# A two-layer hybrid trunk on one core: merges as 512-column products, a beginning by quarters, and overlapping GLA heads

## The chip, the cores and the metric

The kernel runs on one core of a Trainium2 chip, alone. The metric is the device time of one execution in microseconds (us): the median of several runs.

## The reference

The reference is the backbone of a diffusion generator, two layers deep, over 256 context tokens and 256 latent tokens of width 1024. Each layer normalises and modulates its input, projects it once, feeds three mixers that run in parallel, merges them by gates, and ends with an MLP:

```python
def modulate(x, g, shift, scale):
    return rms_norm(x, g) * (1 + scale) + shift
# a layer: one input projection, split into
#   x, y             -> RG-LRU: conv, sigmoid gates, a scan in each direction, times gelu(y)
#   q, k, v, r, z    -> GLA: 4 heads, chunks of 64, both directions; decay gates from z
#   q, k, v          -> attention with 8 query and 2 key/value heads, rotary
#   gates            -> sum over branches of sigmoid(gate_b) * (branch_b @ W_b)
# then an output projection, a gated residual, and a squared-ReLU MLP
    u = jnp.sqrt(-jnp.expm1(2.0 * log_a)) * (i * xc)          # RG-LRU
    scores = jnp.einsum('nbhid,nbhjd->nbhij', qc * jnp.exp(b - b_mid), kc * jnp.exp(b_mid - b))   # GLA
```

Shift and scale come from a product of the conditioning vector with `mod_w`. Only the latent tokens of the last layer are output.

## The kernel before, in words

**Products.** Activations lie transposed: 128 channels on the partitions, up to 512 tokens in the columns (0 to 255 context, 256 to 511 latent). Each fp32 matrix is split into a high part rounded to the matmul's format and the rest, so that each product is three: high by high, high by low, low by high. `weight` loads a 128x1024 tile of weights, casts the high part on ACT (L200, `wh`) and subtracts on DVE (L201, `wl`), two or three weights ahead. `gemm` makes one 128-row output of 8 blocks, 24 products in a PSUM tile `mm`, of which there are four. `gemm_pair` takes an activation whose high and low parts lie beside each other, 256 columns each, so that one 512-column product makes two of the three, and a 256-column product the third; the two halves of its output must be added afterwards. `gemm_tok` makes GLA's V with tokens on the partitions, in four `mm` tiles at once.

**Order.** The scheduler issues each engine's instructions in the order in which the program calls them, but for pieces raised by a priority (weights, transfers of `mod_w`). Every engine then goes through its list in order: an instruction that waits holds up all that stand behind it on its engine. Layer 0 computes all 512 tokens; in layer 1 (`last`) the query side has only the 256 latent columns (`c0` is 256).

**A layer's beginning.** For layer 0 the norm's shift and scale come in four quarters (`mod_half`): a transfer of 2 MB (`mod_load`), products in `mx` tiles, a copy on ACT, a transpose, then an addition on DVE into `modT` (L319). `norm_apply` then makes two of the eight input blocks, from which the first products of the layer start.

**RG-LRU.** Eight blocks of 128 channels, in pairs: `lru_conv`, `lru_gates` (four products L526, activations L527 and L531), `lru_decay` (L538), one square root over a pair (L630), and `lru_scan` on DVE (L545 to L555, with a cast on ACT by L293 behind it). In between stand products of y (`gate_y`).

**GLA.** `gla_z` makes z (L568, with its weight split in `wzs`, L294). `gla_gates(h)` makes the head's log decays from z: products L598, then on ACT L601, L604 (exp) and L605 (ln). `gla(h)` makes K and Q (copied out by L653 and L656), V, then for each direction: exponentials, multiplications on DVE (L677 to L710), scores (L715, L717), and the state's update; a transpose of the decayed K waits for a copy (L775 for L767); R's products and the head's result (L851 follows L841) come last. `merge(b, i)` multiplies one block of a branch's output with its weight, computes the gate's product, and adds (L787 to L792); the merges of branch 1 and 2 in layer 1 have 256 columns.

Which gla step stands where is written out in the program: before, the gates of head 0 come after the last pair's scan, K, Q and V of each head at that head's beginning.

Of the kernel before, what the change touches and what calls it, by code (L numbers as in the profile page):

```python
# [15 lines left out]
F32 = mybir.dt.float32  # L16
# [14 lines left out]
WSPB, EBB, G2B, WRB = 3, 1, 3, 3  # L31
# [6 lines left out]
GZP, G0P = 2, 6  # L38
# [66 lines left out]
def trunk_kernel(ctx: ExitStack, tc: tile.TileContext, out: bass.AP, d: dict):  # L105
# [48 lines left out]
    c8 = const.tile([128, KT, 2], F32, name="c8")  # L154
# [9 lines left out]
    pick = const.tile([128, 2, 32], F32, name="pick")  # L164
    G.memset(pick, 0.0)
    for b in range(2):
        G.memset(pick[:, b, b:b + 1], 1.0)
# [6 lines left out]
    th = const.tile([128, KT, 2], F32, name="th")  # L174
# [100 lines left out]

    def gemm_tok(l, c, hh, hl, ts):
# [44 lines left out]
    def mods(l, us, pace, nd=KT):  # L321
# [5 lines left out]
        def load(u, j, k):  # L327
            with tc.high_priority(M_A):
                t = tmp()
                nc.sync.dma_start(t, d["mod_w"][l, u][:, k, 512 * j:512 * j + 512])  # L330
            return t
# [9 lines left out]
        for u, j in halves:  # L341
            bs = (0, 1) if l == 0 or u < 2 else (1,)
            acc = [tmp() for _ in bs]
            terms = [(pick[:, b, :], a) for a, b in zip(acc, bs)]
# [22 lines left out]
    def mod_load(l, u, h, tag):  # L367

        t = yp.tile([128, KT, 2, 256], F32, name="modw", tag=tag)
        src = d["mod_w"][l, u]  # L370
        if u < 2:
            nc.sync.dma_start(t, src.rearrange("p k (h c) -> p k h c", h=2)[:, :, :, 256 * h:256 * h + 256])
        else:
            nc.sync.dma_start(t.rearrange("p k h c -> p k (h c)"), src[:, :, 512 * h:512 * h + 512])
        return t

    def mod_half(l, u, h, t):
        dsts = (4 * u + 2 * h, 8 + 4 * u + 2 * h) if u < 2 else (8 * u + 4 * h, 8 * u + 4 * h + 2)
        for _ in mod_cols(l, 128, lambda k: (cs[:, k, :], lambda c: t[:, k, c // 256, c % 256:c % 256 + 128]), KT,
                          dsts):  # L380
            pass
# [55 lines left out]

    hn1 = norm_mul(0, 1)
    mq = [mod_load(0, q // 2, q % 2, ("yh", "yl")[q % 2]) for q in range(WQ)]
    first = [weight(0, "in", O_LY + 128 * i, hi="V", ahead=0) for i in range(2)]  # L440
    mq += [mod_load(0, q // 2, q % 2, ("yh", "yl")[q % 2]) for q in range(WQ, 4)]
    st = norm_stats(x1, 0)
    for q in range(4):
        mod_half(0, q // 2, q % 2, mq[q])
        norm_apply(0, 1, x1, 0, T, st, hn1, range(2 * q, 2 * q + 2))


    c2 = const.tile([128, NL, 2, 16], F32, name="c2")
    lam = const.tile([128, NL, 16], F32, name="lam")
    la = const.tile([128, NL, 16], F32, name="la")  # L450
    lb = const.tile([128, NL, 16], F32, name="lb")
    lc = const.tile([128, NL, 16], F32, name="lc")
    lo_, hi_ = PCOLS["lam"]
    V.tensor_copy(lam, par[:, :, lo_:hi_])
    S.activation(la, lam, AF.Abs)
    S.activation(la, la, AF.Exp, scale=-1.0)
    V.tensor_scalar(lb, la, 2.0, None, op0=ALU.add)
    V.reciprocal(lb, lb)
    V.tensor_tensor(la, la, lb, op=ALU.mult)
    V.tensor_tensor(lb, la, la, op=ALU.mult)  # L460
    V.tensor_scalar(lc, lb, 1.0 / 17, 1.0 / 15, op0=ALU.mult, op1=ALU.add)
    for n in (13, 11, 9, 7, 5, 3, 1):
        V.tensor_tensor(lc, lc, lb, op=ALU.mult)
        V.tensor_scalar(lc, lc, 1.0 / n, None, op0=ALU.add)
    V.tensor_tensor(lc, lc, la, op=ALU.mult)
    V.tensor_scalar(lam, lam, -1.0, 0.0, op0=ALU.mult, op1=ALU.max)
    V.scalar_tensor_tensor(lam, lc, 2.0, lam, op0=ALU.mult, op1=ALU.add)
    V.tensor_scalar(c2[:, :, 0, :], lam, -4.0, None, op0=ALU.mult)
    V.tensor_scalar(c2[:, :, 1, :], lam, 2.0, None, op0=ALU.mult)


    habx = const.tile([128, NL, 32], F32, name="habx")
    lo_, _ = PCOLS["ab"]
    _, hi_ = PCOLS["xb"]
    V.tensor_scalar(habx, par[:, :, lo_:hi_], 0.5, None, op0=ALU.mult)

    for l in range(NL):
# [22 lines left out]
        def gate_y(i):  # L500
            w = first[i] if l == 0 and i < 2 else weight(l, "in", O_LY + 128 * i, hi=E_LYH)
            ps = gemm(w, hh, hl, c0)
            ge[i] = x[:, i, :256] if last else tmp()
            S.activation(ge[i], ps, AF.Gelu_apprx_tanh)
# [52 lines left out]

        def gla_z():


            wz = tmp1(F32, (128, KT, 32))
            nc.sync.dma_start(wz, d["wz"][l])
            wzs = t2.tile([128, KT, 64], F32R, name="wzs", tag="t2")
            split_to(wzs[:, :, :32], wzs[:, :, 32:], wz)
# [50 lines left out]

        LYS = LYS0, LYS1
# [29 lines left out]
        v2 = {}  # L646

        def gla(h):
            bs = gla_gates(h) if h else gates0

            pk = gemm(weight(l, "in", O_GK + 128 * h), hh, hl, 0)
            k_ = tmp()
            cp(E_K)(k_, pk)  # L653
            pq = gemm(weight(l, "in", O_GQ + 128 * h), hh, hl, c0)
            q_ = tmp()
            S.activation(q_[:, c0:], pq, AF.Copy, scale=128.0 ** -0.5)  # L656
            if h % 2 == 0:
                for t, ps in gemm_tok(l, O_GV + 256 * h, hh, hl, range(4)).items():
                    for a in range(2):
                        v2[h + a, t] = tmp1()  # L660
                        cp(E_V)(v2[h + a, t], ps[:, 256 * a:256 * a + 256])
            v_ = [v2.pop((h, t)) for t in range(4)]

# [4 lines left out]
            pts, qhs = [], []  # L668
            for dd in range(2):
# [59 lines left out]
                kt = tmp()  # L729
                if dd == 0:  # L730
                    cp(E_KT)(kt[:, :384], pkt[:, :384])
                else:
                    S.copy(kt[:, :256], pkt[:, :256])
                    S.copy(kt[:, 384:], pkt[:, 384:])
                cur = None
# [32 lines left out]
            for j in range(2):  # L768
                pr = gemm(weight(l, "in", O_GR + 256 * h + 128 * j), hh, hl, c0)
                y = tmp()  # L770
                S.activation(y[:, c0:], pr, AF.Tanh, scale=0.5)
                V.scalar_tensor_tensor(y[:, c0:], y[:, c0:], 1.0, pr, op0=ALU.add, op1=ALU.mult)
                po = mx()
                for t in range(t0, 4):
                    P.transpose(po[:, 128 * t:128 * t + 128], on[t - t0][:, 128 * j:128 * j + 128], ident)  # L775
                V.scalar_tensor_tensor(y[:, c0:], po[:, c0:], hg[:, j:j + 1], y[:, c0:],
                                       op0=ALU.mult, op1=ALU.mult)
                split_to(y2h[:, 2 * h + j, c0:], y2l[:, 2 * h + j, c0:], y[:, c0:])
# [171 lines left out]
        def pair(t):  # L950

            return lambda k: t.t[:, k, :].rearrange("p (a b) -> p a b", a=2)
# [185 lines left out]
```

## Time and profile before

| what | value |
|---|---|
| median of three runs | 1898.92 us (1896.93 to 1903.13) |
| the profiled execution | 1897.52 us, span 1895.7 us |
| mean granted TensorE clock | 0.989 |
| PE busy | 1810.9 us, 96% |
| DVE busy | 1282.9 us, 68% |
| ACT busy | 924.8 us, 49% |
| POOL busy | 57.1 us, 3% |

PE is the TensorE's matmul, DVE the VectorE, ACT the ScalarE, SP the engine that issues the transfers. Busy is the time in which an engine had an instruction under way. The idle time of PE is the span less its busy time, and a product at a lower granted clock takes longer while PE still counts as busy. The time of an execution is its span and some 2 us around it.

### The profile page before, as it was taken

To read this page: it belongs to the slowest core of one execution; us is meant where nothing else is said; L and a number is where in the kernel's file an instruction comes from. 1 tells how busy PE (TensorE), PEld (TensorE's weight loads), DVE (VectorE), ACT (ScalarE), POOL (GpSimd) and SP (SyncE) were. 2 spreads that over 40 slices of the span, in tenths; PEclk is the share of its full clock that TensorE was granted. 3 is DMA by queue.
4 is the path that set the end of the run, shared out by engine and by line. 5 is a ranking of instruction groups with operands and counts; after the bars stand their busy time and mean duration, and the time that the engine had idled before them with its cause. 6 is when DMAs were issued, how large, how long until landed. Compare 5 with 4: busy or idle time off the path is not lost.

```text
span 1895.7 us, 26828 instructions
## 1 busy us (share of the span) xinstructions
PE 1810.9 (96%) x10248; PEld 1509.6 (80%) x10248; DVE 1282.9 (68%) x2177; ACT 924.8 (49%) x1586; POOL 57.1 (3%) x88
## 2 busy tenths in 40 slices
PE   5998999999999999999999999996999999999999
PEld 4765778887777888988888889764888878998887
DVE  5677764535566767789744448787765668577877
ACT  3778544334434333564232325876654554455443
POOL 1000000000000000000000001000000000000000
PEclk9999999999999999999999999998999999999999
DMA  9322223222211566666633335531343333664664
GB/s 318 99 74 73 69 69 90 77 93 78 72 51 56 190 193 196 222 224 199 211 109 97 98 102 185 164 114 61 130 122 111 122 123 91 234 193 150 190 190 154
DMA packets 91617, 255.62 MB, mean 135 GB/s; under 512 B 9184, under 2 KB 20576, under 8 KB 91488
## 3 DMA queue, kind: packets, MB, share of 16 engines
q1 hardware_dynamic: 91488, 253.90, 42.6%
q8 instruction: 81, 1.33, 0.3%
q14 instruction: 48, 0.39, 0.1%
HBM read 252.82 MB, written 1.05 MB: 134 GB/s over the span
## 4 chain that ended last, share of the span: by engine, by line
issue 49%; PE 39%; DVE 5%; ACT 4%; POOL 2%; DMA 0%; SPq 0%; POOLq 0%; ACTq 0%; DVEq 0%
PE mm L212 31%; PE mx L212 2%; PE mx L760 1%; PE mx L741 1%; DVE wl L201 1%; ACT wh L200 1%; PE mx L715 1%; PE mx L526 1%; POOL t L425 1%; PE mx L216 1%; DVE lru L546 0%; PE mx L717 0%; DVE lru L545 0%; ACT lru L630 0%; ACT lru L527 0%
## 5 line engine op out<-in xcount | busy, mean ns | idle before, releaser
L212 PE MATMUL mm<-h,wh 128*128 128x512 f32 (+1 forms) x2640 | 733.3, 360 | 8.3 <-DVE wh L198 4.5
L200 ACT CAST wh<-wraw 128x1024 fp32r<-128x1024 f32 x363 | 379.8, 1049 | 544.3 <-PE mm L212 465.3
L201 DVE TENSOR_TENSOR wl<-wraw,wh 128x1024 fp32r<-128x1024 f32 x365 | 445.8, 1223 | 257.6 <-ACT wh L200 254.2
L212 PEld LDWEIGHTS mm<-h,wh 128*128 128x128 f32 x2640 | 468.3, 189 | 85.4 <-issue 6.6
L212 PE MATMUL mm<-h,wl 128*128 128x512 f32 (+1 forms) x1448 | 493.2, 341 | 0.0
L212 PEld LDWEIGHTS mm<-h,wl 128*128 128x128 f32 x1448 | 273.8, 189 | 31.9 <-issue 1.4
L212 PE MATMUL mm<-yh,wh 128*128 128x512 f32 (+1 forms) x640 | 224.7, 351 | 2.4 <-DVE big L957 2.4
L212 PE MATMUL mm<-yh,wl 128*128 128x512 f32 (+1 forms) x640 | 224.3, 350 | 0.0
L212 PE MATMUL mm<-yl,wh 128*128 128x512 f32 (+1 forms) x640 | 222.6, 348 | 0.0
L212 PE MATMUL mm<-wh,h 128*128 128x512 f32 x576 | 187.3, 400 | 18.5 <-ACT t L653 18.1
L212 PE MATMUL mm<-yp,wh 128*128 128x256 f32 (+1 forms) x704 | 186.0, 338 | 3.8 <-ACT g L787 2.3
L212 PE MATMUL mm<-yp,wl 128*128 128x256 f32 x512 | 144.4, 282 | 0.0
L356 DVE SCALAR_TENSOR_TENSOR t<-t,cs,t 128x512 f32<-128x512 f32 x178 | 127.2, 746 | 24.1 <-DMA t<-mod_w 15.1
L212 PEld LDWEIGHTS mm<-wh,h 128*128 128x128 f32 x576 | 109.7, 191 | 42.3 <-ACT t L653 18.9
L212 PEld LDWEIGHTS mm<-yp,wh 128*128 128x128 f32 x704 | 120.8, 191 | 20.1 <-ACT g L787 2.5
L212 PEld LDWEIGHTS mm<-yh,wh 128*128 128x128 f32 x640 | 121.6, 190 | 17.8 <-issue 3.4
L212 PEld LDWEIGHTS mm<-yh,wl 128*128 128x128 f32 x640 | 121.2, 189 | 15.3 <-issue 0.7
L212 PEld LDWEIGHTS mm<-yl,wh 128*128 128x128 f32 x640 | 121.2, 189 | 15.0 <-issue 0.5
L212 PE MATMUL mm<-wl,h 128*128 128x512 f32 x288 | 115.2, 400 | 2.0 <-DVE wl L201 2.0
L212 PEld LDWEIGHTS mm<-yp,wl 128*128 128x128 f32 x512 | 97.1, 190 | 1.0 <-issue 1.0
L212 PE MATMUL mx<-t,t 128*128 128x128 f32 (+2 forms) x416 | 81.8, 338 | 0.0
L957 DVE SCALAR_TENSOR_TENSOR big<-mm,modT,big 128x256 f32<-128x256 f32 x64 | 28.6, 480 | 66.8 <-PE mm L212 66.8
(226 smaller groups left out, 1987.4 us busy)
## 6 DMA issues: line engine op xcount, KB each, us to landing
wraw<-wt SPq DMA_DIRECT2D x365, 512.0 KB, 3.6
t<-mod_w SPq DMA_DIRECT2D x144, 256.0 KB, 3.8
modw<-mod_w SPq DMA_DIRECT2D x6, 2048.0 KB, 14.1
big<-xt SPq DMA_DIRECT2D x8, 512.0 KB, 5.3
gw<-lruw SPq DMA_DIRECT2D x16, 256.0 KB, 3.5
out<-big SPq DMA_DIRECT2D x8, 128.0 KB, 2.5
t<-glaw SPq DMA_DIRECT2D x8, 96.0 KB, 3.1
t<-ropeg SPq DMA_DIRECT2D x2, 256.0 KB, 3.0
```

The lines of the kernel that those rows point to most:

```text
L200: S.copy(wh, r)
L201: (G if lo == "G" else V).tensor_tensor(wl, r, wh.bitcast(F32), op=ALU.subtract)
L212: P.matmul(o, a, b, **kw)
L216: P.transpose(o, a, ident)
L356: V.scalar_tensor_tensor(a, t, c, a, op0=ALU.mult, op1=ALU.add)
L425: G.tensor_tensor(h[:, :n], x[:, k, c0:c1], st[1][:, :n], op=ALU.mult)
L526: P.matmul(pg, gw[:, 2 * dd + q, :], xc, start=True, stop=True)
L715: P.matmul(psc[:, c], en[:, c], em[:, c], start=True, stop=True)
L741: P.matmul(pu[:, :256], kt[:, 128 * t:128 * t + 128], v_[t], start=True, stop=True)
L760: P.matmul(po[:, :256], a, b, start=j == 0, stop=j == len(mm) - 1)
L957: V.scalar_tensor_tensor(x[:, i, c], ps[:, 256 * s - a:256 * s - a + 256], s0[:, i, s:s + 1], x[:, i, c], op0=ALU.mult, op1=ALU.add)
```

## The change

Three things are changed in one step.

**Merges.** In layer 1 the merges of the branches 1 and 2 (the second and third) take `gemm_pair` for both products, with a new helper that adds the halves: a copy on ACT and an addition on DVE. There are 2 branches x 8 blocks x 2 products.

```diff
+    def added(dst, ps):
+        S.copy(dst, ps[:, 256:])
+        V.tensor_tensor(dst, ps[:, :256], dst, op=ALU.add)
+        return dst
...
         def merge(b, i, yh, yl):
-            pb = gemm(weight(l, "br", b, i), yh, yl, c0)
-            pg = gemm(weight(l, "in", O_BG + 1024 * b + 128 * i), hh, hl, c0)
             g = gtmp()
+            if last and b:
+                pb = added(g[:, :256], gemm_pair(weight(l, "br", b, i), pair(yh), 1))
+                pg = added(g[:, 256:], gemm_pair(weight(l, "in", O_BG + 1024 * b + 128 * i),
+                                                 lambda k: hn1[4][:, k, :, 256:], 0))
+            else:
+                pb = gemm(weight(l, "br", b, i), yh, yl, c0)
+                pg = gemm(weight(l, "in", O_BG + 1024 * b + 128 * i), hh, hl, c0)
```

**Beginning.** `mod_w` lies in memory so that each transfer reads contiguous runs of 16 KB, and three products of the first layer are issued in quarters, as the norm's quarters come, between the products of the modulation. Constants of the RG-LRU gates (the softplus of `lam`) are computed after the first `lru_conv` instead of before the layer.

```diff
+    first_ps = [ps_mm.tile([128, 512], F32, name="mm") for _ in range(3)]
...
     for q in range(4):
-        mod_half(0, q // 2, q % 2, mq[q])
+        for i in range(2) if q else ():
+            first_gemm(i, q - 1)
+        g = mod_half(0, q // 2, q % 2, mq[q])
+        next(g)
+        if q:
+            first_gemm(2, q - 1)
+        run(g)
         norm_apply(0, 1, x1, 0, T, st, hn1, range(2 * q, 2 * q + 2))
...
         lru_conv(0)
+        if l == 0:
+            gate_consts()
```

On PE, at the layer's very beginning, the modulation's products (`mx<-modw,cs`, a quarter each) stood before the change like this, with the first gemm's products (`mm<-h,wh`) behind the second quarter:

```order
L212 MATMUL mx<-modw,cs 32x128 x32
L216 MATMUL mx<-ident,t_228 128x128
L212 MATMUL mx<-modw,cs 32x128 x32
L212 MATMUL mm<-h,wh 128x512 x2
L216 MATMUL mx<-ident,t_280 128x128
L212 MATMUL mm<-h,wl 128x512
```

After it the second quarter stands behind twelve of the first gemms' products:

```order
L210 MATMUL mx<-modw,cs 32x128 x32
L214 MATMUL mx<-ident,t_236 128x128
L210 MATMUL mm<-h,wh 128x512 x2
L210 MATMUL mm<-h,wl 128x512
L210 MATMUL mm<-h,wh 128x512 x2
L210 MATMUL mm<-h,wl 128x512
L210 MATMUL mm<-h,wh 128x512 x2
L210 MATMUL mm<-h,wl 128x512
L210 MATMUL mm<-h,wh 128x512 x2
L210 MATMUL mm<-h,wl 128x512
L210 MATMUL mx<-modw,cs 32x128 x32
```

What moved: the second quarter goes behind the products that need only the first; the third and fourth come after 30 and 36 products of the first gemms instead of 31 and 39.

**GLA.** K and Q of head 0 come before the gates of the LRU's block 6, the GLA gates and V of head 0 before those of block 7, and R of head 0 before the last pair's scan. z's weight is split at the layer's start. For heads 1 to 3: gates, K and Q, then the end of the head before (its transposes, scaling and split), V, R. The state's update stands behind the preparation of both directions. The last end comes behind attention's K and V projection.

```diff
             lru_conv(i + 1)
-            lru_gates(i)
             if i < 6:
+                lru_gates(i)
                 lru_conv(i + 2)
+            else:
+                kq0 = gla_kq(0)
+                lru_gates(i)
+                gates0 = gla_gates(0)
+                v0 = gla_v(0)
             lru_gates(i + 1)
...
+            if i == 6:
+                ys0 = gla_r(0)
             for j in range(2):
                 lru_scan(i + j)
             if i == GZP:
                 zs = gla_z()
-            if i == G0P:
-                gates0 = gla_gates(0)
...
+            if h:
+                bs = gla_gates(h)
+                k_, q_ = gla_kq(h)
+                before()
+                v_ = gla_v(h)
+                ys = gla_r(h)
```

On ACT, at the end of layer 0's LRU, the copies of K and Q (L653, L656; `t_1323` and `t_1356`) stood behind the pair's square root, the exponentials of the GLA gates, three loads of ACT's function tables and a cast (L293) of the scan's result `lru`:

```order
L630 ACT_TABLE_LOAD
L630 ACTIVATE lru<-lru,epsc 128x2048
L601 ACTIVATE eb<-mx,par 128x512 x2
L604 ACT_TABLE_LOAD
L604 ACTIVATE eb<-eb 128x1024
L605 ACT_TABLE_LOAD
L605 ACTIVATE eb<-eb 128x1024
L293 CAST yh<-lru 128x512
L653 COPY t_1323<-mm 128x512
L656 ACTIVATE t_1356<-mm 128x512
```

After the change they (L651 and L654 there) stand ahead of the last pair's gates (L554, L558), between casts of the pair before:

```order
L539 ACTIVATE t_1193<-mm,par 128x512
L301 CAST yh<-lru 128x512
L198 CAST wh<-wraw 128x1024
L651 COPY t_1229<-mm 128x512
L198 CAST wh<-wraw 128x1024
L654 ACTIVATE t_1262<-mm 128x512
L301 CAST yh<-lru 128x512
L554 ACTIVATE lru<-mx,par 128x512 x2
L558 ACTIVATE lru<-lru,c_483 128x512
```

What moved: the copies that free K's and Q's PSUM tiles are out of the queue behind the square root and the scan.

On DVE, in layer 1, head 0's preparation of the second direction (its first row is L677) stood before the change when the last pair's scans were over, among weight splits (L201) and the state's update (L746):

```order
L702 TENSOR_TENSOR t_10995<-t_11008,dec 128x2x64
L721 COPY_PREDICATED t_11023<-masks,mx 128x256
L731 COPY t_11030<-mx 128x384
L677 TENSOR_TENSOR t_11044<-eb 128x512
L201 TENSOR_TENSOR wl<-wraw,wh 128x1024
L746 SCALAR_TENSOR_TENSOR t_11038<-t_11034,decp,mx 128x256
L689 TENSOR_TENSOR t_11044<-t_10796,t_11044 128x512
```

After it the last pair's scans (L572 to L582, on `lru`) stand between the first direction's preparation and the second's. From the second direction's first row (L739, 23 rows above this piece) to the last that its scores need (L771, 6 rows below it) stand 41 instructions:

```order
L199 TENSOR_TENSOR wl<-wraw,wh 128x1024
L302 TENSOR_TENSOR yp<-lru,yp 128x256
L578 SCALAR_TENSOR_TENSOR lru<-lru 128x256
L783 COPY_PREDICATED t_11090<-masks,mx 128x256
L581 TENSOR_TENSOR lru<-lru 128x256
L793 COPY g_11097<-mx 128x384
L582 TENSOR_TENSOR lru<-lru,big 128x256
L751 TENSOR_TENSOR t_11099<-t_10704,t_11099 128x512
L302 TENSOR_TENSOR yp<-lru,yp 128x256
L753 COPY t_11107<-t_11099 128x256
L757 TENSOR_TENSOR decp<-dec 128x4
```

What moved: head 0's first direction is prepared ahead of the last pair's scans, and its second direction behind them.

## Rows read from the trace of the kernel before

**Rows 1.** The page's busy times, shares of the span and instructions.
```profile
PE 1810.9 (96%) x10248; PEld 1509.6 (80%) x10248; DVE 1282.9 (68%) x2177; ACT 924.8 (49%) x1586; POOL 57.1 (3%) x88
```

**Rows 2.** Windows: from:to, length, busy PE PEld DVE ACT POOL, clock, DMA, GB/s.
```profile
100.00:150.00 50.00, 47.35 (x180) 32.93 (x179) 34.96 (x50) 36.02 (x49) 0.00 (x0) 0.97 0.25 80
150.00:200.00 50.00, 40.64 (x157) 29.90 (x155) 41.37 (x60) 36.26 (x44) 0.57 (x2) 0.93 0.17 53
200.00:250.00 50.00, 47.92 (x233) 39.28 (x234) 36.46 (x61) 30.69 (x59) 2.48 (x6) 1.00 0.27 86
1250.00:1300.00 50.00, 43.81 (x188) 29.69 (x187) 41.59 (x65) 35.06 (x50) 0.00 (x0) 0.95 0.38 121
1300.00:1350.00 50.00, 38.77 (x188) 29.98 (x188) 37.61 (x66) 31.16 (x51) 1.00 (x4) 0.87 0.26 79
1350.00:1400.00 50.00, 43.85 (x289) 39.64 (x289) 36.94 (x71) 27.57 (x55) 2.58 (x6) 0.93 0.37 118
1620.00:1650.00 30.00, 30.00 (x253) 30.00 (x252) 16.82 (x23) 12.13 (x17) 0.00 (x0) 1.00 0.78 285
```

**Rows 3.** Waits of PE, 50 to 520 us: total, times, longest.
```profile
PE mm L212 <- ACT t L653: 7.6, 1, 7.6
PE mx L775 <- DVE t L767: 3.8, 4, 1.0
PE mx L568 <- DVE wzs L294: 2.6, 1, 2.6
PE mx L715 <- DVE t L709: 2.5, 2, 1.3
```

**Rows 4.** Waits of PE, 1180 to 1600 us, the same columns.
```profile
PE mm L212 <- ACT t L653: 11.9, 2, 10.4
PE mx L526 <- DVE t L515: 4.1, 1, 4.1
```

**Rows 5.** Timeline, end of layer 0's LRU: start, duration, instruction, idle before.
```profile
178.50 2.01 ACT L630 ACTIVATE lru<-lru,epsc 128x2048 f32<-128x2048 f32 x1
...
189.46 0.58 ACT L653 COPY t<-mm 128x512 f32<-128x512 f32 x1
```

**Rows 6.** Windows of 10 us around the same place in layers 0 and 1.
```profile
190.00:200.00 10.00, 9.81 (x36) 7.66 (x36) 9.43 (x16) 3.70 (x6) 0.57 (x2) 0.85 0.01 2
1310.00:1320.00 10.00, 1.73 (x4) 1.44 (x5) 10.00 (x17) 6.44 (x9) 0.00 (x0) 0.63 0.01 2
1320.00:1330.00 10.00, 9.32 (x35) 7.22 (x35) 9.63 (x15) 4.51 (x7) 0.19 (x1) 0.86 0.10 26
```

**Rows 7.** Timeline of PE in layer 0's head 1, dense 512-column products.
```profile
244.65 0.61 PE L212 MATMUL mm<-h,wh 128*128 128x512 f32 x2
...
245.33 0.61 PE L212 MATMUL mm<-h,wh 128*128 128x512 f32 x2
```

**Rows 8.** Timelines: merges of layer 1 (L787, L792), and gemm_pair in its MLP (L993).
```profile
1666.93 0.43 DVE L792 TENSOR_TENSOR big<-big,g 128x256 f32<-128x256 f32 x1
...
1676.73 0.38 ACT L787 ACTIVATE g<-mm 128x256 f32<-128x256 f32 x1
...
1682.49 0.38 ACT L787 ACTIVATE g<-mm 128x256 f32<-128x256 f32 x1
...
1740.49 0.36 ACT L993 COPY g<-mm 128x256 f32<-128x256 f32 x1
...
1743.27 0.36 ACT L993 COPY g<-mm 128x256 f32<-128x256 f32 x1
```

**Rows 9.** Timeline of the beginning.
```profile
22.05 0.42 PE L216 MATMUL mx<-ident,t 128*128 128x128 f32 x1 [0.39 <-ACT t L307]
...
22.42 1.96 PE L212 MATMUL mx<-modw,cs 128*32 128x128 f32 x64
...
24.70 0.22 DVE L319 TENSOR_TENSOR modT<-mx,par 128x4 f32<-128x4 f32 x2
...
28.89 0.99 PE L212 MATMUL mm<-h,wh 128*128 128x512 f32 x2 [4.52 <-DVE wh L198]
```

More of the change, by code (lines that the diff above doesn't have):

```diff
@@ L153, in trunk_kernel @@
     G.memset(cs, 0.0)
-    c8 = const.tile([128, KT, 2], F32, name="c8")
+    c8, th = (tmp1(shape=(128, KT, 2)) for _ in range(2))
     nc.sync.dma_start(c8, d["cs"])
@@ L161, in trunk_kernel @@
     G.memset(epsc, 1e-30)
-    pick = const.tile([128, 2, 32], F32, name="pick")
+    pick = const.tile([128, 33], F32, name="pick")
     G.memset(pick, 0.0)
-    for b in range(2):
-        G.memset(pick[:, b, b:b + 1], 1.0)
+    G.memset(pick[:, 1:2], 1.0)
     def pc(l, name, a=0, n=None):
@@ L438, in trunk_kernel @@
     hn1 = norm_mul(0, 1)
-    mq = [mod_load(0, q // 2, q % 2, ("yh", "yl")[q % 2]) for q in range(WQ)]
-    first = [weight(0, "in", O_LY + 128 * i, hi="V", ahead=0) for i in range(2)]
-    mq += [mod_load(0, q // 2, q % 2, ("yh", "yl")[q % 2]) for q in range(WQ, 4)]
+    first = [weight(0, "in", O_LY + 128 * i, ahead=0) for i in range(2)]
+    mq = [mod_load(0, 0, 0, "yh")]
+    first.append(weight(0, "in", O_LY + 256, ahead=0))
+    mq += [mod_load(0, q // 2, q % 2, ("yh", "yl")[q % 2]) for q in range(1, 4)]
@@ L443, in trunk_kernel @@
     for q in range(4):
-        mod_half(0, q // 2, q % 2, mq[q])
+        for i in range(2) if q else ():
[5 more added lines that the diff above has]
+        run(g)
         norm_apply(0, 1, x1, 0, T, st, hn1, range(2 * q, 2 * q + 2))
+    for i in range(3):
+        first_gemm(i, 3)
     c2 = const.tile([128, NL, 2, 16], F32, name="c2")
-    lam = const.tile([128, NL, 16], F32, name="lam")
@@ L450, in trunk_kernel @@
[L450 to L472, printed above, removed]
@@ L500, in gate_y @@
         def gate_y(i):
-            w = first[i] if l == 0 and i < 2 else weight(l, "in", O_LY + 128 * i, hi=E_LYH)
-            ps = gemm(w, hh, hl, c0)
+            if l == 0 and i < 3:
+                ps = first_ps[i]
+            else:
+                ps = gemm(weight(l, "in", O_LY + 128 * i, hi=E_LYH), hh, hl, c0)
             ge[i] = x[:, i, :256] if last else tmp()
@@ L614, in gla_gates, with gla_kq, gla_v, gla_r @@
             return bs
+        v2 = {}
+        def gla_kq(h):
+            pk = gemm(weight(l, "in", O_GK + 128 * h), hh, hl, 0)
+            k_ = tmp()
+            cp(E_K)(k_, pk)
+            pq = gemm(weight(l, "in", O_GQ + 128 * h), hh, hl, c0)
+            q_ = tmp()
+            S.activation(q_[:, c0:], pq, AF.Copy, scale=128.0 ** -0.5)
+            return k_, q_
+        def gla_v(h):
+            if h % 2 == 0:
+                for t, ps in gemm_tok(l, O_GV + 256 * h, hh, hl, range(4)).items():
+                    for a in range(2):
+                        v2[h + a, t] = tmp1()
+                        cp(E_V)(v2[h + a, t], ps[:, 256 * a:256 * a + 256])
+            return [v2.pop((h, t)) for t in range(4)]
+        def gla_r(h):
+            ys = []
+            for j in range(2):
+                pr = gemm(weight(l, "in", O_GR + 256 * h + 128 * j), hh, hl, c0)
+                y = gtmp()
+                S.activation(y[:, c0:], pr, AF.Tanh, scale=0.5)
+                V.scalar_tensor_tensor(y[:, c0:], y[:, c0:], 1.0, pr, op0=ALU.add, op1=ALU.mult)
+                ys.append(y)
+            return ys
         LYS = LYS0, LYS1
@@ L644, in trunk_kernel, with gla @@
         y2h, y2l = ytiles("yl")
[L646 to L662, printed above, removed]
+        def gla(h, before=None):
+            if h:
[4 more added lines that the diff above has]
+                ys = gla_r(h)
+            else:
+                bs, (k_, q_), v_, ys = gates0, kq0, v0, ys0
             lo = c0 // 64
@@ L734, in gla @@
                     S.copy(kt[:, 384:], pkt[:, 384:])
+                kts.append((kt, decp))
+            for dd, (kt, decp) in enumerate(kts):
+                seq = (0, 1, 2, 3) if dd == 0 else (1, 0, 3, 2)
                 cur = None
@@ L836, in trunk_kernel @@
             av.append(a)
+        end()
         rsk = sm.tile([128, 8], F32, name="rsk")
```

100 lines of the change are left out of this document (62 added, 38 removed).

## The prediction, made before the changed kernel ran

> **What bounds the kernel now.** I read the busy times first, then windows of 50 us, PE's waits in the stretches that stand out, and the timeline at the longest wait. PE is busy 1810.9 us, 96% of the span [rows 1]: idle time is small, and the reader is to see in the windows where it sits. Between 100 and 250 us (end of layer 0's LRU, heads 0 and 1 of its GLA) PE is busy 47.35, 40.64 and 47.92 of 50 us, at a granted clock of 0.97, 0.93 and 1.00; between 1250 and 1400 us, the same place in layer 1, 43.81, 38.77 and 43.85 at 0.95, 0.87 and 0.93 [rows 2]. Such clocks are mixtures of the two levels, 1.2 and 2.4 GHz. Idle time and clock together cost 14.1 + (47.35 x 0.03 + 40.64 x 0.07) = 18.4 us in layer 0 and 23.6 + (43.81 x 0.05 + 38.77 x 0.13 + 43.85 x 0.07) = 34 us in layer 1. That is what the overlap of the GLA heads can win at most in these places.
>
> The waits name it. In layer 0: 7.6 us once for the copy of K (L653), 2.6 for z's split weight, 3.8 in four pieces before the transposes of the decayed K, 2.5 in two for the scores' inputs [rows 3]. In layer 1: 11.9 us for L653, 10.4 of them at once, and 4.1 for the last pair's convolution [rows 4]. L653 is late since ACT takes the pair's square root at 178.50 (2.01 us), then table loads and exponentials, and copies K only at 189.46 [rows 5]; PE needs K's `mm` tile for V. But DVE is nearly full at the same places: 9.43 of 10 us in layer 0, 10.00 and 9.63 in layer 1, where the clock falls to 0.63 and is still at 0.86 in the window behind the wait [rows 6].
>
> **The change part by part.** The sum is made against the profiled execution, 1897.5 us; the median of the runs, 1898.9, lies 1.4 above it.
>
> *Merges.* Merges of two 24-product gemms come every 1682.49 - 1676.73 = 5.76 us, 2.88 a gemm; a `gemm_pair` in layer 1's MLP every 1743.27 - 1740.49 = 2.78 us [rows 8]. The saving is some 0.105 us, times 2 x 8 x 2 = 32: -3.4 us. Added are two copies on ACT (0.36 each, as L993) and two additions on DVE (0.43 each, as L792) per merge [rows 8], 0.7 and 0.9 us in 5.6. DVE has 16.82 of 30 us busy there and ACT 12.13 [rows 2], so the additions hide under the products; if that cover were gone they would cost their 0.9 us a merge. Only behind the last merge do they lengthen a chain on which the output projection waits: +0.5. Bounds: +0.5 (half the saving, and two such tails) to -4.5 (0.14 a gemm, if the weight loads, busy 30.00 of 30 us [rows 2], were the limit before).
>
> The rows give 2.88 us for 24 products of 256 columns. The Trainium skill ("TensorE: Matmul & The Clock Gate", section "Back-to-back issue gap") states a warm gap of N/2.4 + 2.5 ns; estimated from it, 24 x 109 = 2.62 us stand against 8 x (216 + 109) = 2.60, so this part would bring 0.6 us and the additions would be for nothing. The trace doesn't agree: a product takes 2.88/24 = 0.12 us here, and the rows decide.
>
> *Beginning.* Before, the first quarter's transpose is made at 22.05, but its `modT` only at 24.70, because DVE was in the constants of `lam`; the first gemm starts at 28.89. The second quarter's product is made at 22.42, ahead of it [rows 9]. Now the constants are gone from there, so the first gemm can begin near 27. But the second quarter's product stands behind twelve products of the first quarter, which at half the clock take about twice the 0.68 / 3 = 0.227 us of dense ones [rows 7]: it starts at 27 + 12 x 0.45 = 32 at the latest, some 8 to 10 us later. The first gemms' other quarters follow it or their transfers, and their 72 products end about where they did: I take +1. Bounds: +3 (what the second quarter loses is not made up, and the constants delay the first gates) to -4 (the transfers of contiguous memory land earlier, and the 2 us of `modT` count too).
>
> *Layer 0, LRU and GLA.* The copies of K and Q leave the queue behind the square root and the scan, V and R fill the time of the last pair, and z's weight is ready before it is wanted. So I set the whole 18.4 us as gone, and look for what is late next. Walking ACT's and DVE's lists forward with the durations of the trace, the first direction's second scores wait about 4.5 us, because the exponential for them stands on ACT behind the square root and the tanh of R, and the second direction's scores about 4 us, because the scans of the last pair stand ahead of their inputs on DVE. That leaves 8.5: net -10. Bounds -16 (2 us left) to -5 (a third wait as long, before head 1, whose products K, Q, V and R are partly used up as cover).
>
> *Layer 1, LRU and GLA.* The same waits leave, up to 34 us. But Q's and R's products have 256 columns here, half the cover, and DVE is the limit: from the second direction's first instruction to its last input of the scores stand 41 instructions, with the last pair's scans and six weight splits among them. At 10.00 us for 17, as in the window that was full [rows 6], they take 24 us. PE has for that time R (2 x 2.88 us), the first direction's scores and a few transposes. The walk gives waits of 4.5 us (V's second weight behind the convolution's DVE work), 1, 3 and 1, then 11.5 before the second direction's scores, 9 and 3 in head 1: 33 against 34, net -1. Bounds: -10 (a third of these is hidden after all) to +6 (none is, and the clock is down behind the long ones).
>
> *Later heads.* For heads 1 to 3 gates, K and Q come ahead of the end of the head before, and the state's update behind both directions. This covers most of the waits of L775 (3.8 us) and L715 (2.5) [rows 3] that lie behind 250 us, about 4 us; as V and R no longer stand between the last sum and the transposes of its head, I take half, -2. Bounds 0 to -5 with layer 1's.
>
> Sum: -3.4 + 0.5 + 1 - 10 - 1 - 2 = -14.9, from 1897.5 to 1882.6; on the runs' median 1884.
>
> **The rivals.** About 0.3%, 5.7 us, is what a measurement of this kernel can tell from no change.
>
> *Rival 1, the overlap pays in layer 1 too.* If the weight splits are far enough ahead and the products of V and K fill DVE's 24 us, layer 1 leaves 18 of its 34 us and the time is 1884 - 15 = 1869. For it: over 1250 to 1400 us DVE has 41.59, 37.61 and 36.94 of 50 us busy [rows 2], so there is room to move its work forward. Against it: its windows of 10.00 and 9.63 just where it is waited for [rows 6].
>
> *Rival 2, it pays nowhere.* DVE's chain from the square root to head 0's scores sets the end in both layers, the waits only change their names: layer 0 gives -3, layer 1 and the later heads nothing, the beginning +2, the merges -2.9: -4, 1895. For it speaks DVE's 9.43 [rows 6] in layer 0; against it that the wait there was for ACT, whose queue the change clears [rows 5].
>
> *Rival 3, slower.* One mechanism in both layers: DVE comes to head 0's second direction only behind the last pair's scans, so its scores, which stand ahead of all else on PE, wait for what is left of 24 us of DVE work, and head 1's scores behind the same delay once more. In layer 1, with some 10 us of products beside it, that is 14 + 14 us, 6 more for products at the low clock that the 0.86 behind the long wait shows [rows 6], and the other waits of the walk, 9.5: 43.5 against 34, +9.5. In layer 0 R's two gemms cover 2 x 24 x 0.227 = 10.9 us instead of 5.8, which leaves 9 + 9 and the 4.5 for the exponential: 22.5 against 18.4, +4. With the merges' -2.9 and the beginning's +1 the run is 11.6 slower, 1910. It decides where the new waits of both layers together pass 60 us (the 52.4 that are lost now, the 1.9 and the 5.7).
>
> The Trainium skill (same page, section "Why this matters for your kernels") tells to avoid idle gaps between bursts of products, since the clock drops behind them. The trace agrees: 0.63 in the window with the longest wait.
>
> **How the numbers follow.** Forecast (layer 0 pays, layer 1 doesn't) 0.50, its own range 1876 to 1892; rival 1 0.24; rival 2 0.16; rival 3 0.10. The predicted time is the forecast's, 1884. The range of 1864 to 1897 takes in rivals 1 and 2 and the bounds of layer 0 and layer 1 one at a time; outside lie rival 3 and the far ends of the others, just under 2 in 10. Faster by over 0.3%, below 1893.2: the forecast, rival 1 and little of rival 2, 0.75; within 0.3%: 0.15; slower: rival 3, 0.10.
>
> **What would show it.** Merges: the activation L787 every 5.55 us instead of 5.76 in layer 1's dense merges, and no wait named for the new copies or additions. Beginning: the first gemm near 27, the second quarter's product at 30 to 32, dense products from about the same time as before. Layer 0: no wait for K's copy, and in its place 3 to 13 us for head 0's scores; layer 0's windows of 100 to 250 us lose 8 to 9 us instead of 18.4. Layer 1: the wait for K's copy gone, and waits for DVE of 8 to 14 us before head 0's second direction and 5 to 12 before head 1's scores. The prediction would be wrong if layer 0's place didn't lose at least 5 us less, or if layer 1's lost over 10 us less or over 6 more.

## The result and the profile after

The changed kernel takes 1878.64 us (median of four runs, 1874.06 to 1880.38), the kernel before 1900.49 on the same occasion. The ratio is 0.9882, with a 95% interval from 0.9856 to 0.9909: some 22 us, or 1.2%, faster, and inside the range given (1864 to 1897). A second measurement of the same kernel gave 0.9878 (0.9859 to 0.9897).

The page's busy times after, beside [rows 1]:

```profile
PE 1804.1 (96%) x9992; PEld 1500.2 (80%) x9992; DVE 1287.3 (69%) x2206; ACT 937.5 (50%) x1620; POOL 66.5 (4%) x87
```

The span fell from 1895.7 to 1872.3 us, by 23.4. PE has 256 matmuls and 6.8 busy us less (one 512-column product takes the place of two), so most of the gain is idle time. To see where it went, take four marks on PE that both kernels have: the first gate products of the LRU and the first transposes of attention's K, in each layer. These are PE's timeline rows before, and then after:

```profile
65.12 3.60 PE L526 MATMUL mx<-t,gw 128*128 128x512 f32 x8
...
476.21 0.72 PE L851 MATMUL mx<-ident,t 128*128 128x128 f32 x3 [1.45 <-DVE t L841]
...
1200.39 3.67 PE L526 MATMUL mx<-t,gw 128*128 128x512 f32 x8
...
1529.04 0.72 PE L851 MATMUL mx<-ident,t 128*128 128x128 f32 x3 [1.45 <-DVE t L841]
```

```profile
68.83 3.59 PE L553 MATMUL mx<-t,gw 128*128 128x512 f32 x8
...
461.67 0.53 PE L923 MATMUL mx<-ident,t 128*128 128x128 f32 x2 [1.35 <-DVE t L913]
...
1185.67 2.74 PE L553 MATMUL mx<-t,gw 128*128 128x512 f32 x6
...
1507.70 0.52 PE L923 MATMUL mx<-ident,t 128*128 128x128 f32 x2 [1.41 <-DVE t L913]
```

The differences of neighbouring marks give five stretches. The beginning is 3.7 us longer; layer 0's LRU and GLA takes 392.8 instead of 411.1 us (-18.3); the rest of layer 0 is the same (724.0 and 724.2); layer 1's LRU and GLA takes 322.0 instead of 328.7 (-6.6); from there to the end it is 364.6 instead of 366.7 (-2.1). These stretches are used below for every kernel.

PE's waits after, over the LRU and GLA of layer 0 (50 to 520 us, total, times, longest), beside [rows 3], and of layer 1 (1160 to 1600 us), beside [rows 4]:

```profile
PE mx L627 <- ACT lru L554: 2.8, 1, 2.8
PE mx L923 <- DVE t L913: 1.4, 1, 1.4
PE mx L777 <- DVE t L772: 0.8, 1, 0.8
PE mx L777 <- DVE t L771: 0.7, 1, 0.7
```

```profile
PE mx L777 <- DVE t L771: 13.2, 2, 9.6
PE mx L777 <- DVE t L772: 4.0, 1, 4.0
PE mm L210 <- ACT t L651: 3.3, 1, 3.3
PE mx L553 <- ACT lru L565: 1.7, 1, 1.7
```

In layer 0 the waits for K's copy, for z's weight and for the decayed K are gone, and only 2.8 us came in their place, for the gates of block 6 on ACT. In layer 1 the wait for K's copy has turned into waits for the scores' inputs (L771, L772). The windows (columns as in [rows 2]) say the same of the places that [rows 2] show. They are set 15 us earlier, since layer 1 begins 14.7 us earlier; in layer 0, where nothing is won before them, the windows from 100 to 250 us give the same 5.0 us:

```profile
85.00:135.00 50.00, 50.00 (x200) 36.19 (x200) 41.87 (x59) 36.35 (x45) 0.00 (x0) 1.00 0.24 74
135.00:185.00 50.00, 47.15 (x186) 35.67 (x185) 34.97 (x49) 38.58 (x49) 0.00 (x0) 0.97 0.28 90
185.00:235.00 50.00, 49.29 (x231) 39.37 (x230) 38.65 (x60) 29.39 (x46) 3.06 (x4) 1.00 0.29 90
```

```profile
1235.00:1285.00 50.00, 48.33 (x210) 36.00 (x211) 45.85 (x72) 41.58 (x56) 0.00 (x0) 1.00 0.42 137
1285.00:1335.00 50.00, 40.38 (x236) 33.98 (x235) 37.73 (x64) 30.10 (x49) 3.24 (x4) 0.90 0.37 111
1335.00:1385.00 50.00, 39.15 (x235) 35.54 (x235) 32.25 (x64) 24.60 (x49) 2.71 (x6) 0.83 0.24 80
```

By the prediction's reckoning layer 0 loses 3.6 us of idle time and 1.4 by the clock, 5.0 instead of 18.4; layer 1 loses 22.1 and 10.7, 32.8 instead of 34. The windows of layer 1 don't hold quite the same work: 681 products after the change, 665 before.

### The profile page after: what moved, and what is told of

The parts are those of the page before. It is cut to its first block, busy times and chain, and to the rows that moved or that the text cites. A ratio compares the mean times of both kernels' runs of the same rounds, so it can differ in the third digit from the quotient of the medians.

```text
span 1872.3 us, 26339 instructions
## 1 busy us (share of the span) xinstructions
PE 1804.1 (96%) x9992; PEld 1500.2 (80%) x9992; DVE 1287.3 (69%) x2206; ACT 937.5 (50%) x1620; POOL 66.5 (4%) x87
## 4 chain that ended last, share of the span: by engine, by line
PE 30%; issue 21%; DVE 4%; ACT 3%; POOL 1%; POOLq 0%; ACTq 0%; DVEq 0%
PE mm L210 25%; PE mx L210 2%; DVE wl L199 1%; PE mx L806 1%; PE mx L825 1%; ACT wh L198 1%; PE mx L553 0%; PE mx L214 0%; DVE lru L573 0%; POOL t L432 0%; ACT lru L554 0%; ACT lru L699 0%; PE mx L777 0%; DVE lru L572 0%; DVE lru L575 0%
## 5 line engine op out<-in xcount | busy, mean ns | idle before, releaser
L210 PEld LDWEIGHTS mm<-h,wh 128*128 128x128 f32 x2512 | 452.9, 190 | 93.0 <-ACT h L301 9.1
L210 PE MATMUL mm<-yp,wh 128*128 128x512 f32 (+1 forms) x576 | 183.8, 374 | 3.4 <-ACT t L651 3.3
L364 DVE SCALAR_TENSOR_TENSOR t<-t,cs,t 128x512 f32<-128x512 f32 x178 | 127.0, 744 | 24.5 <-DMA t<-mod_w 16.0
L210 PEld LDWEIGHTS mm<-yp,wh 128*128 128x128 f32 x576 | 105.8, 192 | 22.9 <-ACT t L651 3.5
```

The lines of the kernel that those rows point to most:

```text
L210: P.matmul(o, a, b, **kw)
L364: V.scalar_tensor_tensor(a, t, c, a, op0=ALU.mult, op1=ALU.add)
```

## The experiments

Each kernel was timed beside the kernel before; two of them have a single execution. The table has the stretches of its profiled execution in us, and the ratio to the kernel before.

| kernel | first gates | layer 0 LRU, GLA | layer 1 LRU, GLA | to the end | ratio, 95% interval |
|---|---|---|---|---|---|
| before | 65.1 | 411.1 | 328.7 | 366.7 | 1 |
| changed | 68.8 | 392.8 | 322.0 | 364.6 | 0.9882 (0.9856 to 0.9909) |
| merges alone | 67.3 | 409.6 | 328.2 | 369.6 | 0.9985 (0.9975 to 0.9995) |
| beginning alone | 66.9 | 409.7 | 328.3 | 369.7 | 0.9999 (0.9987 to 1.0011) |
| GLA alone | 63.4 | 393.0 | 322.2 | 366.6 | 0.9853 (0.9825 to 0.9881) |
| scans late | 67.1 | 394.5 | 320.1 | 369.0 | 0.9861 (0.9846 to 0.9877) |
| modulation first | 64.7 | 392.8 | 322.1 | 364.5 | 0.9881 (0.9862 to 0.9901) |
| gates early | 66.9 | 396.3 | 318.2 | 365.5 | 0.9884 (0.9860 to 0.9907) |
| z alone | 68.1 | 407.6 | 321.0 | 369.9 | one run, 1894.4 us (before: 1900.3) |
| later heads alone | 66.2 | 403.7 | 324.7 | 369.9 | one run, 1890.4 us (before: 1900.3) |
| head 0 in layer 0 only | 68.9 | 392.9 | 317.8 | 367.8 | 0.9855 (0.9841 to 0.9869) |
| the three together | 65.8 | 393.1 | 316.9 | 367.6 | 0.9837 (0.9823 to 0.9852) |
| and K, Q ahead | 65.0 | 392.9 | 316.9 | 364.8 | 0.9830 (0.9811 to 0.9849) |
| changed, again | 69.6 | 392.9 | 322.6 | 368.0 | 0.9878 (0.9859 to 0.9897) |

Two columns scatter without a change of the code they cover: the first by 2 us and more (65.1 and 67.3 in the kernel before and in the merges alone, which begin alike; 63.4 to 68.1 over all five with the old beginning), the last by about 3.3 (364.6 and 368.0 in the changed kernel, see the end). The rest of layer 0, which isn't in the table, scatters too, from 723.5 to 726.6 (724.0 and 726.1 in the changed kernel). The middle columns repeat within 0.6 us where the code is the same, or within 1.5 over the three kernels with the old GLA, and the conclusions rest on these.

**One part each.** The first three kernels have one of the change's three parts, as its diff shows them.

> The kernel before with the merges alone as 512-column products. My theory (32 gemms save 0.105 us each, the tail gives back 0.5): 3 us faster than before, some 1896 to 1898; the activation L787's place in the dense merges comes every 5.55 us. Rival by the counted columns: 0.6 us, no change that can be seen, every 5.2 to 5.3 us both before and now. Rival of the additions as a new wait: PE waits for the helper's DVE addition between merges, 0 to +5 us.

It was 0.15% faster, 2.9 us (1.0 to 4.8 by the interval). The period of L802, the same activation as L787, is 5.55 us as expected, so the rival by the counted columns is out; these are its last two rows on ACT:

```profile
1679.90 0.42 ACT L802 ACTIVATE g<-g 128x256 f32<-128x256 f32 x1 [1.36 <-DVE g L283]
...
1685.45 0.42 ACT L802 ACTIVATE g<-g 128x256 f32<-128x256 f32 x1 [1.36 <-DVE g L283]
```

PE has no wait for the helper there, but in this profile two others came that the kernel before doesn't have: for the low and the high parts of weights, 1.5 us together (PE's waits, 1530 to 1690 us):

```profile
PE mm L212 <- DVE wl L201: 0.8, 1, 0.8
PE mm L212 <- ACT wh L200: 0.7, 2, 0.5
```

So this one profile doesn't show the gain that the ten timed runs show: from attention's transposes to the end of the output projection's last product it takes 174.9 us, the kernel before 175.3. The changed kernel has no such waits there.

> The kernel before with the beginning by quarters alone (layout of the modulation weights, products in quarters, constants of the gates later). From the trace of the changed kernel I now expect it to be 3 to 4 us slower than before (first gate products at 68.8 instead of 65.1). Rival: the lag at the beginning is given back by the emptied DVE and the earlier transfers later in layer 0, then it is within 1 us of before.

No change of time, within 2.5 us: the loss expected from one profile isn't borne out by the timed runs, and the rival fits them. A first gate product at 66.9 against 65.1 is within what the first column scatters.

> The kernel before with the overlap of the GLA heads alone (and small constants in temporaries, which frees the memory for the fourth buffer). If the three parts add up: 22 to 25 us faster than before, about 1875; 18 to 22 of these in layer 0 and 5 to 7 in layer 1. Rival: the overlap needs the first part of the layer to be as it is in the changed kernel (the constants of the gates late), then under 18 us.

28 us faster (23 to 33 by the interval), so the GLA part alone gains at least what the three parts gain together. Its two LRU and GLA stretches are those of the changed kernel within 0.3 us; the rival is out. The times don't add up, though. The expected 22 to 25 us fit a plain sum only with the loss at the beginning that the run above doesn't show; with 2.9 us for the merges and none for the beginning the three parts come to 31 us, where the changed kernel has 22 to 23. By the profiles GLA alone is ahead of it mainly at the beginning (63.4 against 68.8 and 69.6), in the column that scatters. Whether the quarters cost the changed kernel some us that the beginning alone doesn't show stays open.

**The scans late.** In the changed kernel DVE's list had the last pair's scans in front of head 0's second direction. Here they are called behind it:

```diff
-            for j in range(2):
+            for j in range(2) if i < 6 else ():
                 lru_scan(i + j)
...
+            if h == 0:
+                for i in (6, 7):
+                    lru_scan(i)
+                y2.extend(ytiles("yl"))
             for dd, (kt, decp) in enumerate(kts):
```

> The changed kernel with the last pair's two scans called behind head 0's preparation of both directions, in both layers. My theory, that DVE's list with the scans ahead of the second direction sets layer 1's 9.6 us wait: the wait goes under 2 us and what follows in head 1 (3.3, 4.0, 3.6) shrinks by at least half, 8 to 14 us faster than the changed kernel, ratio to before about 0.983. Rival: ACT's exponentials behind the square root set it; then the wait stays at 6 us or more and the time within 3 us of the changed kernel. Second rival: the scans only move, and head 1's scores wait for them instead; total within 3 us.

The long wait went, as these rows of PE's waits show (1296 to 1400 us), but others came:

```profile
PE mx L777 <- DVE t L772: 5.1, 2, 4.2
PE mx L810 <- DVE t L815: 3.9, 1, 3.9
PE mx L777 <- DVE t L771: 3.6, 1, 3.6
PE mm L210 <- ACT t L651: 3.3, 1, 3.3
PE mx L829 <- ACT yp L301: 2.8, 1, 2.8
```

At the place of the 9.6 us PE now waits 0.9 (the smaller of the two for L772). So the order on DVE does make that wait, and ACT's exponentials don't. But the work has to be done somewhere: the state's update (L810) and head 0's output (L829) now wait, and layer 1 gains 1.9 us instead of 8 to 14, while layer 0 loses 1.7. By the ratios the time is 3 to 4 us below the changed kernel's, with intervals that overlap, which is near the second rival. But it is head 0's update and output that wait now, and head 1's waits stay as they were (3.3, 4.2 and 3.6 us, against 3.3, 4.0 and 3.6), so the scans' place doesn't make these.

**The modulation first.**

```diff
     for q in range(4):
-        for i in range(2) if q else ():
-            first_gemm(i, q - 1)
-        g = mod_half(0, q // 2, q % 2, mq[q])
-        next(g)
-        if q:
-            first_gemm(2, q - 1)
-        run(g)
+        run(mod_half(0, q // 2, q % 2, mq[q]))
         norm_apply(0, 1, x1, 0, T, st, hn1, range(2 * q, 2 * q + 2))
     for i in range(3):
-        first_gemm(i, 3)
+        for q in range(4):
+            first_gemm(i, q)
```

> The changed kernel with the first gemms' products called behind all four quarters' modulation products, as before the change; the contiguous layout, the late constants and the rest stay. My theory: the quarters' products now stand too late on PE (the fourth at 46.5 us, though the transfers are done before 39), so that with this order the layer's first gate products come near 62 to 64 us instead of 67 to 69, and the time is 4 to 6 us below the changed kernel. Rival: the first gemms' number bounds the beginning anyway, then the first gate products stay at 66 to 69 us.

The first gates came at 64.7, and at 65.8 and 65.0 in the two later kernels with this order; with the quarters' order they came at 66.9 to 69.6 in six. That is some 3 us in the profiles (65.2 against 68.1 in the mean), less than expected, and the time doesn't show it.

**The next head's gates early.**

```diff
             if h:
-                bs = gla_gates(h)
+                bs = nxt.pop()
...
+            if h < 3:
+                nxt.append(gla_gates(h + 1))
             for dd, (kt, decp) in enumerate(kts):
```

> The changed kernel with the GLA gates of the next head called behind the preparation of this head's second direction, ahead of the state's update. My theory for layer 1's head 1: its scores wait 4.0 + 3.6 us (and its K copy 3.3) because the chain from its gates on is longer than the products beside it; with the gates some 10 us earlier these waits fall from 11 to under 4 us, and the time by 5 to 9 us. Rival: DVE and ACT are busy with head 0 then, so that head 0's state and output are delayed by what head 1 gains; within 2 us of the changed kernel.

In layer 1 it gains 3.8 us (318.2), less than expected: head 1's waits fall from 10.9 to 4.6 us. In layer 0 it loses 3.5 (396.3), and the time is that of the changed kernel, as the rival has it. In layer 0 head 1's scores have no wait to lose, and head 0's output has new ones (2.2 and 0.9 us).

**The GLA part taken apart.** z alone is the kernel before with z's split at the layer's start; the later heads alone are the GLA part with z and head 0 put back.

> The kernel before with z's weight split at the layer's start alone. My theory: it takes away the 2.6 us wait and the low clock behind it, 4 to 5 us in layer 0 between the fourth and the fifth gate products, and 1.4 us in layer 1; the later wait for K's copy stays at 7 to 8 us. Rival: the wait only moves on to the gates of the next pair, then under 2 us.

> The kernel before with heads 1 to 3 overlapped and the state's update behind both directions alone (head 0 and z as before). My theory: the waits of later heads go, 4 to 6 us in layer 0 and 2 to 4 us in layer 1, while the wait for K's copy of head 0 stays (7.6 and 10.4 us). If head 0's overlap is what pays, this has 6 to 10 us of the 25 to 28; rival: the overlap of the later heads is the larger part, 14 us or more.

Against the mean of the three kernels with the old GLA (410.1 and 328.4), z is worth 2.5 us in layer 0 and 7.4 in layer 1, the later heads (with the fourth buffer, which wasn't tried apart) 6.4 and 3.7. The whole part is worth 17.3 and 6.4. What is left for head 0's overlap, by subtraction, is a gain of 8.3 us in layer 0 and a **loss of 4.7 in layer 1**. These shares rest on one profile each; the loss is tested below, the gain in layer 0 isn't.

In layer 0 z alone brings less than expected: the wait for K's copy falls from 7.6 to 3.5 us, but PE stands 4.0 us before a pair's gates instead. In layer 1 z is worth more than its own wait of 1.4 us. The scheduler doesn't keep to the program's order, as the description of the kernel had it. The program calls z's products ahead of the convolutions of blocks 5 and 6; before, with the weight late, they stood behind the two gemms of these convolutions, and with the weight ready they stand in front of them. These are PE's rows of z's first product and of the last pair's first gates, before, and then with z alone:

```profile
1257.09 0.42 PE L568 MATMUL mx<-h,wzs 128*64 128x512 f32 x1 [1.37 <-DVE wzs L294]
...
1296.96 6.33 PE L526 MATMUL mx<-t,gw 128*128 128x512 f32 x8 [4.11 <-DVE t L515]
```

```profile
1244.88 0.39 PE L570 MATMUL mx<-h,wzs 128*64 128x512 f32 x1
...
1294.49 3.70 PE L526 MATMUL mx<-t,gw 128*128 128x512 f32 x8 [0.26 <-DVE t L515]
```

Counted from the layer's first gates, DVE begins the third pair's scans at 76.4 us instead of 82.3. The wait for the last pair's convolution, 4.1 us [rows 4], falls to 0.3, and the eight products behind it take 3.70 us instead of 6.33. How z's place brings the scans forward is read from the order of the rows; no run tries it. The wait for K's copy stays. In PE's waits of layer 1, z alone:

```profile
PE mm L212 <- ACT t L655: 11.8, 2, 10.3
PE mx L777 <- DVE t L769: 2.3, 4, 0.7
PE mm L212 <- ACT g L789: 2.3, 1, 2.3
```

The later heads alone gain 9.9 us in their one execution, as expected, and the rival (14 us or more) is out.

**Head 0 ahead in layer 0 only.** That the parts add up in layer 1 was tested by leaving out the one that costs:

```diff
-            if i < 6:
+            if i < 6 or last:
                 lru_gates(i)
-                lru_conv(i + 2)
+                if i < 6:
+                    lru_conv(i + 2)
             else:
                 kq0 = gla_kq(0)
...
+            elif last:
+                bs, (k_, q_), v_, ys = gates0, gla_kq(h), gla_v(h), gla_r(h)
```

> The changed kernel with head 0's K, Q, gates, V and R ahead of the last pair in layer 0 alone; in layer 1 they stand as before the change (gates behind the last scan, the rest at the head's beginning), with z's weight early and heads 1 to 3 overlapped in both layers. My theory from the runs with one part: in layer 1 z early is worth 7 us and the later heads 4, and head 0 ahead costs some 5 of them, so layer 1's stretch from its first gate products to the end of its GLA takes about 317 to 318 us instead of 322, and the whole 3 to 6 us less than the changed kernel. Rival: the parts overlap (the wait for K's copy, 10.4 us, stays whole when only z is early), so that the stretch takes 320 to 324 us and the time is that of the changed kernel.

Layer 1 took 317.8 us, as the sum says (328.4 - 7.4 - 3.7 = 317.3), with the wait of 10.3 us for K's copy back. The time is 0.23 to 0.27% below the changed kernel's by the ratios; their intervals overlap.

**Together.** This kernel with the modulation first, and the next head's gates early in layer 1 (the two diffs above, the second with `and last`):

> The kernel of the run before this one (head 0 ahead in layer 0 alone) with the modulation's products first at the beginning, and in layer 1 the gates of the next head behind the second direction. If the pieces add up: layer 1's stretch 3 to 4 us shorter once more (314), the beginning 2 to 4, the whole 6 to 10 us below the changed kernel, ratio to before 0.983 to 0.985. Rival: the gates of the next head only take from head 0's output what they give to head 1, then 2 to 4 us in the beginning are all.

0.9837 (0.9823 to 0.9852), clear of both measurements of the changed kernel though not of the GLA part alone, and the ratio that was expected. The pieces didn't add up as expected, though: layer 1's stretch is 316.9 us, 0.9 shorter than in the run before and not 3 to 4, and the beginning is 3.1 shorter. By the stretches the rival has it: in this kernel the early gates bring little. The last attempt was at the remaining wait of 10.3 us:

```diff
             if i < 6 or last:
+                if i == 6:
+                    kq0 = gla_kq(0)
                 lru_gates(i)
```

> The kernel of the best run so far with K and Q of head 0 ahead of the last pair's gates in layer 1 too, but gates, V and R behind, as there. My theory: what is worth having of head 0's overlap in layer 1 is that the copy of K leaves the queue behind the square root; the 10.3 us wait for it goes, V fills the time of the scans, and the scores wait some 3 to 6 us for DVE instead: 3 to 6 us less than the best run, a ratio of 0.981 to 0.983. Rival: DVE's scans and the gates behind them set the first scores however the products stand; then PE waits 8 to 10 us before the scores instead of before V, and the time is that of the best run.

> The changed kernel itself once more, beside the kernel before on the same chip, to place the runs against it: a ratio of 0.987 to 0.990.

The changed kernel again came to 0.9878, as expected. In the kernel with K and Q ahead the wait for K's copy is gone, and the stretch (316.9) and the time are those of the run before: PE now waits 8.8 us for DVE, in front of a product of the next modulation, whose sum (L364) stands behind the scans on DVE. The rival had it, but for the product that waits: here too PE goes on when DVE is through with the scans.

PE's row, and DVE's rows ahead of it:

```profile
1306.50 0.66 PE L210 MATMUL mx<-t,pick 128*32 128x128 f32 x8 [8.82 <-DVE t L364]
```

```profile
1303.33 0.40 DVE L577 TENSOR_TENSOR lru<-lru,big 128x256 f32<-128x256 f32 x1
...
1305.72 1.40 DVE L364 SCALAR_TENSOR_TENSOR t<-t,cs,t 128x512 f32<-128x512 f32 x2
```

## Why the prediction was right, and where its sizes were off

The direction, the range and the main reason are right: the gain is the overlap's, and most of it is in layer 0. The forecast of 1884 was 5 us too high, since the later heads and layer 0 gave more than their terms.

*Merges: right.* -2.9 was forecast. The timed runs of the merges alone have -2.9 (-4.8 to -1.0). In the profiles the changed kernel takes 172.4 us from attention's transposes to the output projection's last product, the GLA part alone 174.8: -2.4. These are the last products, in the changed kernel and in GLA alone, whose first transposes stand at 1507.70 and 1505.30:

```profile
1680.14 0.28 PE L210 MATMUL mm<-yp,wl 128*128 128x256 f32 x1
```

```profile
1680.13 0.28 PE L210 MATMUL mm<-yp,wl 128*128 128x256 f32 x1
```

The period of 5.55 us came as forecast, and the row of 2.88 us per gemm was the right price, not the gap by columns, by which the helper would have been for nothing. In this stream, where every product has a weight load of its own (9992 of each on the page), a product of 256 columns takes 0.12 us and not the 0.109 of that gap.

*Beginning: +1 forecast, about +2 in the profiles, none in the time of the beginning alone (-2.5 to +2.1).* The first gates come at 68.1 us in the mean of the six profiles with the quarters, at 66.0 in the five with the old beginning, which scatter from 63.4 to 68.1. The first gemm (27.17) and the second quarter's product came as worked out; that product is at 32.12. What wasn't seen is that the delay is handed on: the third and fourth quarter's products stand behind the gemms of the one before, at 42.98 and 46.52, though the transfers were nearly over by 41 us. The share of the DMA engines over the first 60 us, in 40 slices of 1.5 us, in tenths:

```profile
DMA  0679999897999989899998999940000000000005
```

PE's rows with the second, the third (its last 60 products) and the fourth quarter:

```profile
32.12 1.95 PE L210 MATMUL mx<-modw,cs 128*32 128x128 f32 x64
...
42.98 1.94 PE L210 MATMUL mx<-modw,cs 128*32 128x128 f32 x60
...
46.52 1.96 PE L210 MATMUL mx<-modw,cs 128*32 128x128 f32 x64
```

*Layer 0: direction right, size too small: -10 forecast, with a part of the later heads' -2; -18.3 measured.* In the windows 18.4 - 5.0 = 13.4 us were won, inside the bounds (-16 to -5). The mis-sized term is "what is late next", 8.5 us: two waits of 4.5 and 4 us before head 0's scores were walked out by hand, and the trace has 0.7 (and 2.8 at another place). The products of K, Q, V and R have 512 columns there, and DVE's scans are done before PE wants their results. The other 5 us lie mostly behind the windows, with heads 2 and 3.

*Later heads: -2 forecast for both layers, bounds 0 to -5; 6.4 and 3.7 us measured.* This is the term that was furthest off. It took half of some 4 us; in the run with the later heads alone the waits of L775 and L715 in layer 0, 6.3 us before, fall to 0.6. By the same runs z and head 0 together bring 10.8 us in layer 0 and 2.7 in layer 1, near the -10 and -1 that were forecast for them.

*Layer 1: -1 forecast, -6.6 measured.* The place itself lost 32.8 us where 33 were walked out, but that the totals meet is luck. The walk's 33 are all waits; measured are 22.1 us of waits and 10.7 at the low clock, which the walk left out. Two of its waits came nearly as forecast, 9.6 us before the second direction's scores (11.5) and 10.9 in head 1 (12); others didn't come. DVE starts the scans when ACT's square root is done, then goes on with a single pause of 0.28 us, scans and weight splits first, and PE follows:

```profile
1308.78 1.29 DVE L572 SCALAR_TENSOR_TENSOR lru<-lru 128x512 f32<-128x512 f32 x2 [3.51 <-ACT lru L699]
...
1327.30 0.68 DVE L751 TENSOR_TENSOR t<-t,t 128x512 f32<-128x512 f32 x1
...
1330.53 0.42 DVE L771 TENSOR_TENSOR t<-t,t 128x256 f32<-128x256 f32 x1
```

By the runs with one part, the gain is 3.7 us in the later heads and 7.4 through z, whose share in layer 1 the prediction didn't price, less the 4.7 of head 0. Rival 1 (the overlap pays in layer 1) is wrong in its reason, since head 0's overlap costs 4.7 us there; rival 3's mechanism is the true one for that piece, at half its price: one long pause came, and head 1's waits, which stay when the scans are moved, aren't behind the same delay. Why the walk lost nothing of V's second weight (4.5 forecast, none seen) wasn't looked into.

## What to carry to other kernels

Before moving a stage's products ahead of a wait, compare how long they last with the work that the other engines have queued at the same time. Here the same overlap won 8.3 us (by subtraction) in the layer where all its products have 512 columns, and cost 4.2 to 4.8 (tested) in the layer where Q's and R's have 256. That the columns make the difference fits the waits, but no run tries it alone. A change of several parts should be taken apart by layer, since a part that loses hides behind one that wins, and the times of the parts should be added up again: here they didn't sum to the whole. And a small operand that is late can be worth more than its own wait: z's weight 7.4 us for a wait of 1.4 in layer 1, though only 2.5 for 2.6 in layer 0.

## What was not expected of the hardware

The same `gemm_pair` ran at two rates. In the MLP of layer 1 it took 2.77 us in some executions and 2.83 in others, with a granted clock of 1.00 in both. These are ACT's copies in the changed kernel, in its first profile and in its second:

```profile
1728.16 0.36 ACT L280 COPY g<-mm 128x256 f32<-128x256 f32 x1
1730.94 0.36 ACT L280 COPY g<-mm 128x256 f32<-128x256 f32 x1
```

```profile
1729.57 0.36 ACT L280 COPY g<-mm 128x256 f32<-128x256 f32 x1
1732.39 0.37 ACT L280 COPY g<-mm 128x256 f32<-128x256 f32 x1
```

It makes some 3.3 us at the end, more than the merges bring, and no run here shows its cause. The merges aren't free of it either: their period is 5.55 us in most profiles, but 5.65 in those of the modulation first and of the gates early, whose MLP ran at 2.77. ACT's rows in the modulation first:

```profile
1645.06 0.42 ACT L852 ACTIVATE g<-g 128x256 f32<-128x256 f32 x1 [1.36 <-DVE g L281]
1650.71 0.42 ACT L852 ACTIVATE g<-g 128x256 f32<-128x256 f32 x1 [1.36 <-DVE g L281]
```
